# Streaming encoder step on one core: first weights laid out by block with their squares summed on TensorE, the norm's columns between a sublayer's first two units, weight splits ordered behind the norm, early gate weights

## The chip, the cores and the metric

The kernel runs on one core of a Trainium2 chip. The metric is the device time of one execution in microseconds (us). Of the kernel before, three runs were timed: 965.52, 967.45 and 967.6 us, median 967.45. One more execution was recorded by the hardware profiler; the trace and its page come from it.

In the text, TensorE is PE in the profile (PEld its weight loads), VectorE is DVE, ScalarE is ACT, GpSimd is POOL, and SP is the engine that issues the loads from memory.

## The reference

One step of a two-layer encoder over 288 tokens (256 of a prompt, 32 of a sample with caches), 1024 features. Each layer has three sublayers, each on a normed copy of the stream `x` and added back to it:

```python
def rmsnorm(x, g):
    xf = x.astype(jnp.float32)
    y = xf * lax.rsqrt(jnp.mean(xf * xf, axis=-1, keepdims=True) + RMS_EPS)
    return (y * g.astype(jnp.float32)).astype(x.dtype)
...
def memory_attn(h, mk, mv, w_q, w_o):
    ...
    return o.reshape(b, t, D_MODEL) @ w_o

def swiglu(h, w_gate, w_up, w_down):
    return (jax.nn.silu(h @ w_gate) * (h @ w_up)) @ w_down
```

In layer 0 the first sublayer is a chunked attention and a stick-breaking attention side by side (`mix_ab`); in layer 1 it is a forgetting attention whose scores get a bias from the cumulated logarithm of 16 gates (`mix_c`). Then come cross-attention into 256 memory tokens (`cross`) and a gated feed-forward part with 22 x 128 hidden features (`ffn`). A last norm gives the output.

## The kernel before, in words

**Layout.** Features lie on the 128 partitions, tokens along the row: `x` is eight tiles of 128 x 288. A weight matrix comes in units of 128 x 1024 (512 KB), eight blocks of 128 x 128. `unit` (L169) loads one through SP into `st` (four buffers) and splits it into a rounded part `hi` (a cast on ScalarE, L150; five buffers) and the rest `lo` (a subtraction on VectorE, L151; four buffers). `mm3` (L178) multiplies each block with the activations, which are split the same way into `hh` and `hl`: hi x hh, hi x hl, lo x hh. So a unit is 24 matmuls over 288 columns.

**The norm.** The scale 1/rms is not applied to the activations before the product but to its result. Class `Norm` sums the squares of the eight blocks of `x`: the squares on ScalarE (`sq`, L235), the additions on POOL, the last one on VectorE (`ssq`, L243). `columns` brings the sum across partitions with six small matmuls (`nrm`), then takes the inverse root by Newton's steps on VectorE (`ms`, `y`, `nt`; 11 small instructions, L257 to L262). `rows` spreads it along the tokens with six more matmuls (`nr`), and `scale` copies it to `rstd` on ScalarE (L310). What is to be scaled (`xq` in cross, `gs` and `us` in ffn, `q`, `kv` and the gate's `gz` in mix_c) waits in a list until then.

**The opening of a sublayer.** `begin` (L194) computes the first six blocks of the first two units, for the last two blocks of `x` aren't there yet. `project` finishes each unit. After each finished unit `tick` advances the generators in `active`, `scale` among them: in cross and ffn it does nothing at the first tick, issues `columns` at the second and `rows` at the third, in the two mix sublayers one tick earlier.

**The order.** A scheduler orders the instructions of each engine; each engine then works through its own list. `not_before` adds an order without a wait. `held` (L165) uses it for the two halves of a split, only while `hurry` is set (the first four heads of mix_ab): they stand behind an earlier matmul and behind what `scale` has put into `behind`. Elsewhere splits run ahead as far as the buffers go.

**The start.** SP loads the first three units (`first`) in nine pieces of columns, between the four pieces of `x`. Their blocks are multiplied side by side, in `side_by_side` (L802), and the eight squares are added on VectorE (seven additions, L243) before one group of `nrm`. 32 matmuls of a unit matrix (`warm`, L132) precede all of this.

**Mix_c.** The gate's 32 weight columns (`wg`) are loaded at the opening, multiplied by the gain on VectorE (`wgg`, L944), and used for `gp`. `gate` (L878) turns this into `gz`, transposes with the summing matrix `fold4` (`gt`), and after a chain of small steps into `lf`, from which matmuls make the cumulated bias (`gc`, `gs`, `gn`); it goes to memory and comes back by loads. For each pair of sample heads `sample` loads four strips of it (`bcs`) and four columns (`cq`), subtracts, and masks four strips on POOL (L989). At the end, `turn_early` puts four transposes between the two halves of the last norm's `nrm`.

Of the kernel before, what the change touches and what calls it, by code (L numbers as in the profile page):

```python
# [26 lines left out]
def encoder_step(ctx: ExitStack, tc: tile.TileContext, a):  # L27
# [46 lines left out]

    first = [wp.tile([P, 1024], F32, tag="st", bufs=4, name=f"first{i}") for i in range(3)]

    def first_part(i, c0, c1):
        DMA.dma_start(first[i][:, c0:c1], a["w_ab"][4 * i][:, c0:c1])

    PARTS = ((0, 256), (256, 512), (512, 1024))  # L80
    first_part(0, *PARTS[0])
    for i in range(4):
        DMA.dma_start(xh[i], a["xT"][:, 2 * i * NT:2 * (i + 1) * NT])
        if i == 0:
            DMA.dma_start(gain, a["gains"])
        if i < 3:
            for u in range(3):
                if i or u:
                    first_part(u, *PARTS[i])
# [16 lines left out]
    V.tensor_copy(ntrir, ntri)  # L106
# [27 lines left out]
    V.tensor_scalar(ident, warm[:, 0:P], 1.0 / 32.0, None, op0=ALU.mult)  # L134
    fold = cst.tile([P, 2, 32], F32, name="fold")
    by_head = ident.rearrange("p (j i q) -> p j i q", j=2, i=2)
    V.tensor_tensor(fold, by_head[:, :, 0], by_head[:, :, 1], ALU.add)

    fold4 = cst.tile([P, 16], F32, name="fold4")
    V.tensor_tensor(fold4, fold[:, 0, 0:16], fold[:, 1, 0:16], ALU.add)  # L140
# [53 lines left out]
    def begin(srcs, h):  # L194
# [30 lines left out]
    class Norm:  # L225
# [7 lines left out]
        def add(self, xb, eng=None):  # L233
# [3 lines left out]
            eng = eng or (V if self.parts == KT else G)  # L237
            i = int(self.parts == KT and self.hurry)
            if self.acc[i] is None:
                self.acc[i] = q  # L240
            else:
                s = tok("ssq")
                eng.tensor_tensor(s[:, :self.n], self.acc[i][:, :self.n], q[:, :self.n], ALU.add)  # L243
                self.acc[i] = s

        def columns(self, between=None):
            p = att("nrm")
            c = len(self.tiles)
            for part in self.acc:
                if between and part is self.acc[1]:  # L250
                    between()
                for i, t in enumerate(self.tiles):
                    if part is not None:
                        mm(p[:, 2 * i:2 * i + 2], part[:, t:t + 128], mean1, i == 0 and part is self.acc[0], False)
# [28 lines left out]
    class Next:  # L283


        def __init__(self, gi):
            self.gi, self.norm, self.h, self.waiting = gi, Norm(hurry=gi == 8), ([], []), []

# [213 lines left out]
    def stick_prompt(q, k, v, vns, j, oh, ol):  # L502
# [121 lines left out]
    def cross(layer, cur, memory, nxt):  # L624
        o = ([tok("oh", F32R) for _ in range(KT)], [tok("ol", F32R) for _ in range(KT)])
        q, qs = [], []
        begun = begin([a["w_xq"][layer, f] for f in range(2)], cur.h)
# [101 lines left out]
    def ffn(layer, cur, nxt, ahead):  # L729
# [16 lines left out]
        begun = begin([a["w_gate"][layer, 0], a["w_up"][layer, 0]], cur.h)  # L746
# [50 lines left out]
    def mix_ab(cur, nxt, memory, w0):  # L797
# [3 lines left out]

        def side_by_side():  # L802
            p = [att("pj"), acc("pj"), acc("pj")]
            with tc.issue_after(warmed.ins):
# [8 lines left out]
        biases = {}  # L813
# [64 lines left out]
    def gate(cur, p, res, lf, bf):  # L878
# [10 lines left out]
        z, e, u, l, f = (sm.tile([P, 48], F32, tag="g" + s, bufs=1, name="gate_" + s) for s in "zeulf")  # L889
# [41 lines left out]

    def mix_c(cur, nxt, memory, w0):
        o = ([tok("oh", F32R) for _ in range(KT)], [tok("ol", F32R) for _ in range(KT)])
        cum = []
        lf = cst.tile([P, 64], F32, name="lf")
        not_before(DMA.dma_start(lf[:, 48:64], a["clf"]), loads[-4])
        bf = cst.tile([P, 1], F32, name="bf")
        G.memset(bf, 0.0)
        not_before(DMA.dma_start(bf[0:16], a["b_f"]), loads[-4])

        wg, wgg = tok("wg"), tok("wgg")
        DMA.dma_start(wg[:, 0:256], a["w_g"])
        g = gain[:, KT:2 * KT].unsqueeze(2).to_broadcast([P, KT, 32])
        V.tensor_tensor(wgg[:, 0:256].rearrange("p (k c) -> p k c", c=32), wg[:, 0:256].rearrange("p (k c) -> p k c", c=32), g, ALU.mult)  # L944
        w = a["w_c"]
        begun = begin([w[0], w[8]], cur.h)
        active.append(cur.scale())
        p = acc("gp")
        for k in range(KT):
            mm(p[32 * (k % 4):32 * (k % 4) + 32, :NT], wgg[:, 32 * k:32 * k + 32], x[k], k < 4, k >= 4)  # L950
# [24 lines left out]
        def sample(g):  # L975
# [11 lines left out]
            for h in range(4):  # L987
                pr = slice(32 * h, 32 * h + 32)
                G.affine_select(out=t[pr, 128:160], in_=t[pr, 128:160], pattern=[[-1, NS]], compare_op=ALU.is_ge,  # L989
                                fill=NEG, base=0, channel_multiplier=1)  # L990
            oo = ([o[0][j] for j in two], [o[1][j] for j in two])
            return attend_sample([qs[j] for j in two], [ks[j] for j in two], two, vns, ck, cv, t, oo)
# [6 lines left out]
    w0 = [unit_tiles() for _ in first]  # L999
    for m in range(KT):  # L1000
        cur.block(m, start=True)
        if m in (1, 3, 5):
            for st, w in zip(first, w0):
                split_weights(st, w, *PARTS[m // 2])
    for m in range(KT):
        cur.norm.add(x[m], V)
    memories = [Memory(0), Memory(1)]
    for layer in range(2):
        nxt = Next(2 + layer)
        (mix_ab, mix_c)[layer](cur, nxt, memories[layer], w0)  # L1010
        cur, nxt = nxt, Next(6 + layer)
# [12 lines left out]
    def turn_early():  # L1024
        for m in range(4):
# [3 lines left out]
    for t in range(3):  # L1029
        for m in range(4 if t == 0 else 0, KT):  # L1030
# [21 lines left out]
def _pack(inputs):  # L1052
# [17 lines left out]
    def vals(c):  # L1070
# [4 lines left out]
                      g["g_ffn"][0], g["g_ffn"][1], g["g_final"]])  # L1075
    w_g = np.pad(g["w_in_c"][0][:, 3072:], ((0, 0), (0, 16)))
# [5 lines left out]
        "w_ab": units(g["w_in_ab"][0]), "w_oab": units(g["w_out_ab"][0]),  # L1082
# [41 lines left out]
```

## Time and profile before

| | |
|---|---|
| runs | 965.52, 967.45, 967.6 us; median 967.45 |
| profiled execution | 965.87 us; span in the trace 964.2 us |
| granted TensorE clock | 0.998 |
| TensorE busy | 946.9 us, 98% of the span, 7484 instructions |
| VectorE, ScalarE, POOL busy | 591.0, 485.7, 239.9 us (61%, 50%, 25%) |
| moved by DMA | 160.99 MB, 167 GB/s on average |

A row of the timeline gives the start and the length in us, the engine, the line of the kernel, the operation, and the tile written and those read, with their shapes; in brackets, how long the engine had been idle before, and what released it. A row of the chain gives start, length, engine and tile. Rows with "x" and a number stand for that many instructions in a row. Consecutive instructions of an engine overlap a little, so the distance between starts, not the length of one, is the pace.

### The profile page before, as it was taken

To read this page: it belongs to the slowest core of one execution; us is meant where nothing else is said; L and a number is where in the kernel's file an instruction comes from. 1 tells how busy PE (TensorE), PEld (TensorE's weight loads), DVE (VectorE), ACT (ScalarE), POOL (GpSimd) and SP (SyncE) were. 2 spreads that over 40 slices of the span, in tenths; PEclk is the share of its full clock that TensorE was granted. 3 is DMA by queue.
4 is the path that set the end of the run, shared out by engine and by line. 5 is a ranking of instruction groups with operands and counts; after the bars stand their busy time and mean duration, and the time that the engine had idled before them with its cause. 6 is when DMAs were issued, how large, how long until landed. Compare 5 with 4: busy or idle time off the path is not lost.

```text
span 964.2 us, 19131 instructions
## 1 busy us (share of the span) xinstructions
PE 946.9 (98%) x7484; PEld 914.2 (95%) x7484; DVE 591.0 (61%) x1140; ACT 485.7 (50%) x862; POOL 239.9 (25%) x364
## 2 busy tenths in 40 slices
PE   8999999999999999999989999999999999999997
PEld 7889999999999999999988899999989999999996
DVE  6786556676766555855466666667767655555442
ACT  5566767544554444444345445455546544444331
POOL 3341122300212222410115454423012222222010
PEclk9999999999999999999999999999999999999999
DMA  8666445443354544555456455545425444444531
GB/s 264 202 206 202 142 170 192 167 159 126 122 171 155 175 163 166 176 197 175 165 187 200 159 191 186 165 169 189 157 85 175 154 173 157 174 164 165 175 110 50
DMA packets 50459, 160.99 MB, mean 167 GB/s; under 512 B 7864, under 2 KB 9336, under 8 KB 50368
## 3 DMA queue, kind: packets, MB, share of 16 engines
q1 hardware_dynamic: 46464, 149.71, 45.7%
q0 software_dynamic: 3904, 10.04, 3.0%
q8 instruction: 59, 0.97, 0.4%
q14 instruction: 32, 0.26, 0.1%
HBM read 149.58 MB, written 10.15 MB: 166 GB/s over the span
## 4 chain that ended last, share of the span: by engine, by line
PE 91%; DVE 3%; DMA 2%; ACT 2%; issue 1%; SPq 0%; POOL 0%; DVEq 0%; ACTq 0%; POOLq 0%
PE pj L68 51%; PE dn L68 14%; PE op L68 10%; PE mv L68 5%; PE po L68 1%; PE xo L68 1%; DMA x<-xT 1%; PE zb L68 1%; PE sc L68 1%; PE xs L68 1%; DMA st<-w_ab 1%; DMA wg<-w_g 1%; PE nrm L68 1%; PE xss L68 1%; ACT hi L150 1%
## 5 line engine op out<-in xcount | busy, mean ns | idle before, releaser
L150 ACT CAST hi<-st 128x1024 fp32r<-128x1024 f32 x257 | 269.1, 1050 | 321.9 <-issue 142.8
L68 PE MATMUL pj<-hh,hi 128*128 128x288 f32 (+1 forms) x1344 | 400.9, 298 | 1.1 <-DVE gz L882 1.1
L68 PE MATMUL pj<-hl,hi 128*128 128x288 f32 (+1 forms) x1344 | 395.6, 294 | 0.0
L68 PE MATMUL pj<-hh,lo 128*128 128x288 f32 (+1 forms) x1344 | 394.7, 294 | 0.4 <-DVE lo L151 0.4
L151 DVE TENSOR_TENSOR lo<-st,hi 128x1024 fp32r<-128x1024 f32 x257 | 321.3, 1250 | 116.8 <-PE dn L68 42.7
L68 PEld LDWEIGHTS pj<-hh,hi 128*128 128x128 f32 x1344 | 253.2, 188 | 7.1 <-issue 5.4
L68 PEld LDWEIGHTS pj<-hh,lo 128*128 128x128 f32 x1344 | 253.3, 188 | 1.1 <-DVE lo L151 1.0
L68 PEld LDWEIGHTS pj<-hl,hi 128*128 128x128 f32 x1344 | 253.3, 188 | 0.5 <-issue 0.5
L68 PE MATMUL dn<-fh,hi 128*128 128x288 f32 x400 | 108.6, 294 | 0.0
L68 PE MATMUL dn<-fh,lo 128*128 128x288 f32 x352 | 103.7, 295 | 0.0
L68 PE MATMUL dn<-fl,hi 128*128 128x288 f32 x304 | 89.4, 294 | 0.0
L68 PE MATMUL op<-ol,hi 128*128 128x288 f32 x256 | 75.7, 296 | 0.0
L68 PE MATMUL op<-oh,hi 128*128 128x288 f32 x256 | 75.5, 297 | 0.0
L68 PE MATMUL op<-oh,lo 128*128 128x288 f32 x256 | 75.2, 294 | 0.0
L68 PEld LDWEIGHTS dn<-fh,hi 128*128 128x128 f32 x400 | 72.5, 188 | 0.0
L68 PEld LDWEIGHTS dn<-fh,lo 128*128 128x128 f32 x352 | 66.1, 188 | 0.0
L243 POOL TENSOR_TENSOR ssq<-ssq,sq 128x288 f32<-128x288 f32 (+1 forms) x35 | 36.3, 1036 | 114.8 <-ACT sq L235 72.3
L742 POOL TENSOR_TENSOR fl<-us,fh 128x288 fp32r<-128x288 f32 x38 | 33.0, 868 | 119.2 <-ACT fh L741 116.6
L738 POOL TENSOR_TENSOR gs<-gs,sg 128x288 f32<-128x288 f32 x44 | 38.7, 880 | 74.7 <-ACT sg L736 73.5
L68 PEld LDWEIGHTS dn<-fl,hi 128*128 128x128 f32 x304 | 57.1, 188 | 0.0
L737 DVE TENSOR_TENSOR us<-pj,rstd 128x288 f32<-128x288 f32 x44 | 20.1, 457 | 59.2 <-PE pj L68 59.2
L68 PEld LDWEIGHTS op<-ol,hi 128*128 128x128 f32 x256 | 48.1, 188 | 0.6 <-issue 0.4
(266 smaller groups left out, 1261.4 us busy)
## 6 DMA issues: line engine op xcount, KB each, us to landing
st<-w_gate SPq DMA_DIRECT2D x44, 512.0 KB, 3.2
st<-w_up SPq DMA_DIRECT2D x44, 512.0 KB, 3.2
st<-w_down SPq DMA_DIRECT2D x44, 512.0 KB, 3.2
st<-w_c SPq DMA_DIRECT2D x24, 512.0 KB, 3.3
st<-w_ab SPq DMA_DIRECT2D x21, 512.0 KB, 4.8
st<-w_xk SPq DMA_DIRECT2D x16, 512.0 KB, 3.4
st<-w_xv SPq DMA_DIRECT2D x16, 512.0 KB, 3.7
st<-w_xq SPq DMA_DIRECT2D x16, 512.0 KB, 3.7
```

Source lines behind the costliest of these rows:

```text
L68: return T.matmul(out, lhsT, rhs, start=start, stop=stop, skip_group_check=True)
L150: a = S.copy(hi, st[:, c0:c1])
L151: b = V.tensor_tensor(lo, st[:, c0:c1], hi.bitcast(F32), ALU.subtract)
L243: eng.tensor_tensor(s[:, :self.n], self.acc[i][:, :self.n], q[:, :self.n], ALU.add)
L737: V.tensor_tensor(us, pu[:, :NT], cur.r, ALU.mult)
L738: G.tensor_tensor(gs, gs, sg, ALU.mult)
L742: G.tensor_tensor(lo, us, hi.bitcast(F32), ALU.subtract)
```

## The change

- **First weights.** The host lays out blocks of the first three units in the order in which they are used (`w_first`): eight steps of three blocks. They come in four loads (of 384, 640, 1024 and 1024 columns) between the pieces of `x`, and are split in seven parts.
- **First norm.** The eight squares are not added: `Norm.sum` puts six `nrm` matmuls for each, from the third step of `side_by_side` on, so that TensorE accumulates them.
- **Columns earlier.** `begin` calls `columns` after the first unit's six blocks, for every sublayer but the first; `scale` issues `rows` at its first tick.
- **Splits held.** `scale` now fills `behind` in every sublayer: first Newton's last step, and one tick later the copy to `rstd` and the last evacuation. `held` orders every split behind the last three entries, for those on its own engine.
- **Gate.** `wg`, `lf`'s cached columns and `bf` are loaded after mix_ab, the multiplication by the gain is on POOL, `gp` takes a bank of the other pool. The five gate tiles are one tile.
- **Mix_c's samples.** Two loads for each pair instead of eight, one addition of a mask made once (`mnew`) instead of four selections, and one tick more before the scores.
- **Small ones.** The two mask matmuls of each `zb` become one; some constants (`ident`, `fold`, `fold4`, `ntrir`) are written later on VectorE; `turn_early` makes two transposes instead of four.

```diff
+    first_part(0, 0, 384)
+    x_part(0)
+    DMA.dma_start(gain, a["gains"])
+    first_part(0, 384, 1024)
+    x_part(1)
+    first_part(1, 0, 1024)
+    x_part(2)
+    first_part(2, 0, 1024)
+    x_part(3)
...
     def held(ins):
-        if hurry[0]:
-            for i in began[-2:-1] + [i for i in behind if i.engine == ins.ins.engine]:
-                not_before(ins, i)
+        for i in (began[-2:-1] if hurry[0] else []) + [i for i in behind[-3:] if i.engine == ins.ins.engine]:
+            not_before(ins, i)
...
             for k in range(BEGIN):
-                mm3(p[:, :NT], w, k, h, k, k == 0, False)
+                mm3(p[:, :NT], w, k, cur.h, k, k == 0, False)
             out.append((w, p))
+            if len(out) == 1:
+                cur.y = cur.norm.columns()
         return out
...
+        def sum(self, p, part, begin):
+            for i, t in enumerate(self.tiles):
+                mm(p[:, 2 * i:2 * i + 2], part[:, t:t + 128], mean1, begin and i == 0, False)
...
         def scale(self):
 
-            if self.gi > 1:
+            if self.gi == 0:
                 yield 1
-            y = self.norm.columns()
-            yield 1
-            p = self.norm.rows(y)
+            p = self.norm.rows(self.y)
...
-            if self.gi == 0:
-                behind.append(self.norm.last.ins)
-                yield 1
-                behind.extend([r.ins, done[-1].ins])
+            behind.append(self.norm.last.ins)
+            yield 1
+            behind.extend([r.ins] + [d.ins for d in done[-1:] if d is not None])
...
-            mm(z[:, 0:128], identb, mdiag, False, False)
-            mm(z[:, 256:384], identb, mdiag, False, False)
+            mm(z[:, 0:512].rearrange("p (t q) -> p t q", q=256)[:, :, 0:128], identb, mdiag.unsqueeze(1).to_broadcast([P, 2, P]), False, False)
...
-                        i = mm3(p[u][:, :NT], w0[u], k, cur.h, k, k == 0, k == KT - 1)
+                        b = 3 * k + u
+                        i = mm3(p[u][:, :NT], w0[b // 8], b % 8, cur.h, k, k == 0, k == KT - 1)
                         if k in (0, 5, 7) and u == 2:
                             began.append(i.ins)
+                    if k > 1:
+                        cur.norm.sum(sums, squares[k - 2], k == 2)
+            for q in squares[KT - 2:]:
+                cur.norm.sum(sums, q, False)
+            cur.y = cur.norm.newton(sums)
...
+    def gate_inputs():
+
+        for t, src in ((lf[:, 48:64], a["clf"]), (bf[0:16], a["b_f"]), (wg, a["w_g"])):
+            not_before(DMA.dma_start(t, src), loads[-1])
+        G.tensor_tensor(wg, wg, gain[:, KT:2 * KT].unsqueeze(2).to_broadcast([P, KT, 32]), ALU.mult)
...
-        begun = begin([w[0], w[8]], cur.h)
+        begun = begin([w[0], w[8]], cur)
         active.append(cur.scale())
-        p = acc("gp")
+        p = att("gp")
...
-            for h in range(4):
-                off = sp.offset + 160 * (4 * g + h)
-                pr = slice(32 * h, 32 * h + 32)
-                DMA.dma_start(t[pr, 0:160], bass.AP(tensor=sp.tensor, offset=off, ap=[[0, NS], [1, 160]]))
-                DMA.dma_start(cq[pr, 0:1], bass.AP(tensor=sp.tensor, offset=off + 128, ap=[[1, NS], [1, 1]]))
+            off = sp.offset + 160 * 4 * g
+            DMA.dma_start(t[:, 0:160], bass.AP(tensor=sp.tensor, offset=off, ap=[[160, 4], [0, NS], [1, 160]]))
+            DMA.dma_start(cq[:, 0:1], bass.AP(tensor=sp.tensor, offset=off + 128, ap=[[160, 4], [1, NS], [1, 1]]))
             G.tensor_tensor(t[:, 0:160], cq[:, 0:1].to_broadcast([P, 160]), t[:, 0:160], ALU.subtract)
...
+            G.tensor_tensor(t[:, 128:160], t[:, 128:160], mnew, ALU.add)
+            yield 1
```

**The order on ScalarE, opening of layer 0's cross.** In the rows before, `hh` and `sq` belong to the last blocks of the projection ahead of it, `rstd` is the norm's copy, `qh` the casts of the first queries, and `hi` the casts of this sublayer's units:

```order
L150 CAST hi_2771<-st_2769 128x1024
L277 ACTIVATE hh_2570<-x_82,gain 128x288
L235 ACTIVATE sq_2574<-x_82 128x288
L150 CAST hi_2838<-st_2836 128x1024
L277 ACTIVATE hh_2610<-x_82,gain 128x288
L235 ACTIVATE sq_2614<-x_82 128x288
L150 CAST hi_2895<-st_2893 128x1024
L150 CAST hi_2975<-st_2973 128x1024
L150 CAST hi_3031<-st_3029 128x1024
L310 COPY rstd_2749<-nr_2745 128x288
L349 CAST qh_2753<-xq_2751 128x256
```

The same place in the changed kernel, from the last blocks' `hh` and `sq` on:

```order
L291 ACTIVATE hh_2565<-x_82,gain 128x288
L243 ACTIVATE sq_2569<-x_82 128x288
L291 ACTIVATE hh_2605<-x_82,gain 128x288
L243 ACTIVATE sq_2609<-x_82 128x288
L323 COPY rstd_2724<-nr_2720 128x288
L156 CAST hi_2746<-st_2744 128x1024
L361 CAST qh_2728<-xq_2726 128x256
L361 CAST qh_2740<-xq_2738 128x256
L156 CAST hi_2783<-st_2781 128x1024
```

Five casts that stood ahead of the copy have moved behind it; `hi_2746` is that of the third unit. VectorE has the same in the changed kernel, with Newton's last step (`y`), the scaled queries (`xq`) and the third unit's `lo_2747`:

```order
L276 SCALAR_TENSOR_TENSOR y_2676<-nt_2677,y_2676 128x6
L656 SCALAR_TENSOR_TENSOR xq_2726<-pj_2652,rstd_2724 128x288
L656 SCALAR_TENSOR_TENSOR xq_2738<-pj_2695,rstd_2724 128x288
L157 TENSOR_TENSOR lo_2747<-st_2744,hi_2746 128x1024
L362 TENSOR_TENSOR ql_2729<-xq_2726,qh_2728 128x256
```

The third unit's `lo` has come to stand behind two queries. **The order on TensorE** at that place in the changed kernel: `nr` is the rows group, `pj_2695` the last two blocks of the second unit, `pj_2750` the third unit, `xs` the scores of the first head:

```order
L68 MATMUL nr_2720<-ident,y_2676 128x128 x2
L68 MATMUL nr_2720<-ident,y_2676 128x32
L68 MATMUL pj_2695<-hh_2565,hi_2691 128x288
L68 MATMUL pj_2695<-hl_2566,hi_2691 128x288
L68 MATMUL pj_2695<-hh_2565,lo_2692 128x288
L68 MATMUL pj_2695<-hh_2605,hi_2691 128x288
L68 MATMUL pj_2695<-hl_2606,hi_2691 128x288
L68 MATMUL pj_2695<-hh_2605,lo_2692 128x288
L68 MATMUL pj_2750<-hh_2377,hi_2746 128x288
L68 MATMUL pj_2750<-hl_2378,hi_2746 128x288
L68 MATMUL xs_2812<-kh_1257,qh_2728 128x256
L68 MATMUL xs_2812<-kl_1258,qh_2728 128x256
```

Between `nr` and the third unit stand the six last matmuls of the second. **At the start**, the end of the side-by-side blocks on TensorE, before:

```order
L68 MATMUL pj_285<-hh_233,hi_185 128x288
L68 MATMUL pj_285<-hl_234,hi_185 128x288
L68 MATMUL pj_285<-hh_233,lo_186 128x288
L68 MATMUL nrm_358<-mean_100,ssq_265 128x2 x3
L68 MATMUL pj_393<-hh_187,hi_389 128x288
```

and in the changed kernel, where `sq` are squares of single blocks of `x`:

```order
L68 MATMUL pj_267<-hl_236,hi_181 128x288
L68 MATMUL pj_267<-hh_235,lo_182 128x288
L68 MATMUL nrm_268<-mean_95,sq_239 128x2 x3
L68 MATMUL nrm_268<-mean_95,sq_241 128x2 x3
L68 MATMUL nrm_268<-mean_95,sq_243 128x2 x3
L68 MATMUL pj_396<-hh_183,hi_392 128x288
```

Five more groups of this kind stand between the earlier steps. Each row with x3 is six matmuls in the trace.

More of the change, by code (lines that the diff above doesn't have):

```diff
@@ L77, in first_part, with x_part @@
     def first_part(i, c0, c1):
[L78 to L82, printed above, removed]
+        DMA.dma_start(first[i][:, c0:c1], a["w_first"][i][:, c0:c1])
+    def x_part(i):
         DMA.dma_start(xh[i], a["xT"][:, 2 * i * NT:2 * (i + 1) * NT])
[L84 to L89, printed above, removed]
+    first_part(0, 0, 384)
[7 more added lines that the diff above has]
+    x_part(3)
     mean1 = cst.tile([P, 2], F32, name="mean1")
@@ L888, in gate @@
         mm(t[0:NS, 32:48], zt[:, 256:288], fold4)
-        z, e, u, l, f = (sm.tile([P, 48], F32, tag="g" + s, bufs=1, name="gate_" + s) for s in "zeulf")
+        five = tok("gate")
+        z, e, u, l, f = (five[:, 48 * i:48 * i + 48] for i in range(5))
         G.memset(z, 0.0)
@@ L934, in mix_c @@
         cum = []
[L935 to L944, printed above, removed]
         w = a["w_c"]
[L946 removed]
+        begun = begin([w[0], w[8]], cur)
         active.append(cur.scale())
[L948 removed]
+        p = att("gp")
         for k in range(KT):
[L950 removed]
+            mm(p[32 * (k % 4):32 * (k % 4) + 32, :NT], wg[:, k], x[k], k < 4, k >= 4)
         cur.then(lambda: start(gate(cur, p, cum, lf, bf)))
@@ L999, in encoder_step, with square @@
     w0 = [unit_tiles() for _ in first]
+    parts = iter([(0, 0, 384), (0, 384, 768), (0, 768, 1024), (1, 0, 512), (1, 512, 1024), (2, 0, 512), (2, 512, 1024)])
+    squares = []
+    def square(m):
+        squares.append(tok("sq"))
+        S.activation(squares[m], x[m], AF.Square)
     for m in range(KT):
         cur.block(m, start=True)
[L1002 to L1006, printed above, removed]
+        for i, c0, c1 in [p for _, p in zip(range((1, 1, 2, 0, 1, 1, 1, 0)[m]), parts)]:
+            split_weights(first[i], w0[i], c0, c1)
+        if m > 1:
+            square(m - 2)
+    square(KT - 2)
+    square(KT - 1)
+    more_constants()
     memories = [Memory(0), Memory(1)]
@@ L1024, in turn_early @@
     def turn_early():
-        for m in range(4):
+        for m in range(2):
             turn(0, m)
@@ L1029, in encoder_step @@
     for t in range(3):
-        for m in range(4 if t == 0 else 0, KT):
+        for m in range(2 if t == 0 else 0, KT):
             turn(t, m)
```

58 lines of the change are left out of this document (35 added, 23 removed).

## The prediction

> **What bounds the kernel now.** I read the table of busy times first, then the chain that ended last, the costliest groups, a stretch in the middle, and TensorE's list of waits.
>
> ```profile
> PE 946.9 (98%) x7484; PEld 914.2 (95%) x7484; DVE 591.0 (61%) x1140; ACT 485.7 (50%) x862; POOL 239.9 (25%) x364
> PE 91%; DVE 3%; DMA 2%; ACT 2%; issue 1%; SPq 0%; POOL 0%; DVEq 0%; ACTq 0%; POOLq 0%
> L150 ACT CAST hi<-st 128x1024 fp32r<-128x1024 f32 x257 | 269.1, 1050 | 321.9 <-issue 142.8
> L151 DVE TENSOR_TENSOR lo<-st,hi 128x1024 fp32r<-128x1024 f32 x257 | 321.3, 1250 | 116.8 <-PE dn L68 42.7
> 280.00:320.00 40.00, 40.00 (x306) 39.98 (x305) 24.60 (x41) 19.85 (x28) 11.09 (x14) 1.00 0.50 169
> 282.44 129.75 PE pj L68 x982
> ```
>
> TensorE is busy for 98% of the span; from 280 to 320 us (the window's row: length, then busy time of PE, PEld, DVE, ACT, POOL, then granted clock) for 40.00 of 40.00 us at clock 1.00. Its pace is 129.75 / 982 = 0.132 us a matmul, so a unit of 24 takes 3.17 us. To split a unit costs ScalarE 1.05 and VectorE 1.25 us: both have room on average. Only two things can move the end: work added to TensorE, and time in which it stands. Standing is rare (each row: who waits for what, us in total, times, longest):
>
> ```profile
> PE warm L132 <- POOL identb masks.py:199: 2.6, 1, 2.6
> PE gp L68 <- DVE wgg L944: 1.3, 1, 1.3
> PE pj L68 <- DVE gz L882: 1.1, 1, 1.1
> PE nrm L68 <- DVE ssq L243: 1.1, 1, 1.1
> PE ts L441 <- DVE es L389: 0.8, 1, 0.8
> PE gc L68 <- DVE lf L904: 0.6, 1, 0.6
> PE nr L68 <- DVE y L262: 0.2, 1, 0.2
> ```
>
> The change goes at nearly every row here. But no row names a wait at the opening of the two cross sublayers and the two ffns, and the change touches those too. Against the profiled execution (965.87 us, span 964.2) I sum six terms.
>
> **1. The start.** Removed: 7 adds on VectorE and the wait behind them, and the waits for the third parts of the weights. Added: 7 more groups of six norm matmuls.
>
> ```profile
> 5.92 0.59 PE L68 MATMUL pj<-hh,hi 128*128 128x288 f32 x1
> 12.25 0.36 PE L68 MATMUL pj<-hh,lo 128*128 128x288 f32 x1
> ...
> 14.52 0.29 PE L68 MATMUL pj<-hh,hi 128*128 128x288 f32 x1
> 15.98 3.27 DVE L243 TENSOR_TENSOR ssq<-ssq,sq 128x288 f32<-128x288 f32 x6
> 19.31 0.83 PE L68 MATMUL nrm<-mean,ssq 128*128 128x2 f32 x6 [1.06 <-DVE ssq L243]
> 20.14 3.51 PE pj L68 x24
> 199.43 0.56 PE nrm L68 x6
> ```
>
> An undisturbed group costs TensorE 0.56 us (0.093 a matmul, for two columns of result), so seven cost 3.9. Gone are the wait of 1.06 and its group's slow start (0.83 - 0.56 = 0.27). Between 12.25 and 14.52 seven steps from matmul to matmul take 2.27 us where 7 x 0.132 = 0.92 would do: the third parts' splits come late there, by 1.35 in all, and those blocks now come in other pieces. I take it that nothing waits in their place except perhaps the first block of the second load (0 to 0.4). TensorE still starts at about 5.92, since the 32 warming matmuls stand before it. Sum: 3.9 - 1.3 - 1.4 = **+1.2**. Bounds: +0.3, if half of the added time falls into waits that come anyway, to +2.0, if the old part waits come back in another place.
>
> The Trainium skill, "TensorE: Matmul & The Clock Gate", section "Back-to-back issue gap", says that the spacing of a stream of weight loads and matmuls is set by both, and gives about 81 ns with 128 columns streamed; by that a group of six, which stream two columns each, would be an estimated 0.49 us at most and the start 0.5 us shorter. The row has 0.56, which I use.
>
> **2. The two cross openings.** Before, `held` ordered splits only in the first four heads. Now each split stands behind the last step of the norm: the cast `hi` behind the copy of rstd on ScalarE, `lo` behind Newton's last step and then the evacuations on VectorE. Before, five casts stood ahead of that copy; now the third unit's comes after it. The norm itself moves up by one unit, so that between the rows matmuls and the third unit TensorE has only six matmuls.
>
> ```profile
> 193.06 6.37 PE pj L68 x48
> 195.03 0.45 DVE L243 TENSOR_TENSOR ssq<-ssq,sq 128x288 f32<-128x288 f32 x1
> 203.18 1.05 ACT L150 CAST hi<-st 128x1024 fp32r<-128x1024 f32 x1 [2.64 <-PE pj L68]
> 203.54 0.66 PE nr L68 x6
> 204.23 0.40 ACT L310 COPY rstd<-nr 128x288 f32<-128x288 f32 x1
> 204.66 1.19 DVE L645 SCALAR_TENSOR_TENSOR xq<-pj,rstd 128x288 f32<-128x288 f32 x3
> ```
>
> Count from the start of the rows matmuls (nr). TensorE: 0.66 + 6 x 0.132 = 1.45, then it wants `hi` of unit 3. ScalarE: rstd starts at 204.23 - 203.54 = 0.69 and takes 0.40, then the cast takes 1.05: ready at about 2.1. Stall 0.6. Then two matmuls of the unit and two of the scores, and TensorE wants `lo`, without stalls at 1.45 + 4 x 0.132 = 1.96. VectorE: the first xq from 204.66 - 203.54 = 1.12; the second needs the end of unit 2's last matmul at about 1.65 and ends at 2.1 (1.19 / 3 = 0.40 each, more when alone); `lo` then takes 1.25: 3.35. All in all 3.35 - 1.96 = 1.4 each: **+2.8**. Bounds 1.0 (`hi` and `lo` overlap with what is ahead of them) to 1.8 each. The sum of squares is no new wait: its last add ended 195.48 - 193.06 = 2.42 us after the projection before, and the 18 matmuls that now stand ahead of nrm take 2.38; a split that delayed that add has moved behind it besides.
>
> **3. The two ffn openings.**
>
> ```profile
> 281.80 0.64 PE nr L68 x6
> 282.48 0.40 ACT L310 COPY rstd<-nr 128x288 f32<-128x288 f32 x1
> 282.89 1.28 ACT L736 ACT_TABLE_LOAD   x1
> 282.91 0.46 DVE L735 TENSOR_TENSOR gs<-pj,rstd 128x288 f32<-128x288 f32 x1
> 283.28 0.45 DVE L737 TENSOR_TENSOR us<-pj,rstd 128x288 f32<-128x288 f32 x1
> ```
>
> The same, with gs and us in place of the two xq and no scores matmuls: `lo` is there at about 3.35, TensorE wants it at 1.45 + 2 x 0.132 = 1.72. Stall **1.65** each, **+3.3**. Bounds 1.3 to 2.0: the table load of 1.28 stands behind the third unit's cast and delays the gate product and so the fourth unit's `lo`, which by the same count is ready within 0.2 of its turn.
>
> **4. Mix_c's opening.** Gone: the waits for wgg (1.3), gz (1.1) and y (0.2), since w_g is loaded and scaled a sublayer earlier, in POOL's idle time, and the copies no longer meet a split. With lf's 0.6 that is 3.2 by the list, 3.7 with the slower matmul after each.
>
> ```profile
> 495.11 0.84 PE nr L68 x6
> 496.40 0.47 DVE gz L882
> 497.94 0.52 PE gt L68 x6
> ```
>
> New: VectorE has gz, q, gz's bias and kv (four of about 0.4 from 1.15, to 2.6), then waits for the gate transposes to copy (to 3.4), then `lo`: ready at 4.65. TensorE wants it at 2.85 (nr, six matmuls, two of unit 3, gt, four of the memory units). Stall 1.8. The gate's chain moves with it and lf stays late by about 0.7. Together 2.5 (2.7 with restarts) against 3.7: **-1.0**. Bounds -2.4 (no stall but lf) to 0.
>
> **5. Mix_c's first sample heads.**
>
> ```profile
> 531.86 1.07 POOL L989 TENSOR_SCALAR_AFFINE_SELECT bcs<-bcs 32x32 f32<-32x32 f32 x4
> 532.96 0.32 DVE L384 CUSTOM_DVE_ANT_0 es<-ss,bcs 128x160 f32<-128x160 f32 x1 [0.36 <-POOL bcs L989]
> 534.44 0.33 PE L441 MATMUL ts<-ident,es 128*128 128x128 f32 x1 [0.77 <-DVE es L389]
> ```
>
> Two loads instead of eight, one add instead of four selects, and a unit more between scores and bias: the wait of 0.77 goes, **-0.8** (bounds -1.0 to 0).
>
> **6. Nothing.** The merged mask matmuls stream the same columns; the constants built later on VectorE are first needed after the start; the gate's tiles and mnew are POOL's work, 25% busy; if POOL's scaling of w_g waited for its load, only the adds of squares would queue behind it, two units ahead of their use. At the tail the last norm matmuls stand behind the same nine transposes.
>
> Sum: 1.2 + 2.8 + 3.3 - 1.0 - 0.8 = **+5.5**. The profiled execution becomes 971.4; it lay 1.6 below the median of the runs shown (967.45, from 965.52 to 967.6). Adding 5.5 to the median gives 973.0; I forecast **972.3** between.
>
> **The rivals.** *A, faster: the openings are covered.* If casts and subtractions of unit 3 got done within the 1.45 us, terms 2 and 3 vanish and the first part of 4: 1.2 - 2.8 - 0.8 = -2.4, 965.1. It decides at a delay from nr to `hi` of 1.45 and to `lo` of 1.72 to 1.96 us; for it, that no opening waits now, and ScalarE idles 2.64 us before the cast at 203.18. Against it, rstd's own row already ends at 1.09 and a cast is 1.05. It needs a queue other than the written one. 0.1.
>
> *B: the start is a gain.* The norm groups fall into time in which TensorE would wait for loads anyway, or cost less between other matmuls: with a third of their 3.9 left, the start is 1.3 - 2.7 = -1.4 in place of +1.2, the total +2.9, 969.7.
>
> ```profile
> 0.00:20.00 20.00, 15.99 (x111) 15.00 (x111) 12.67 (x29) 13.15 (x29) 8.50 (x34) 1.00 0.84 257
> 2.57 3.59 PE L132 MATMUL warm<-identb 128*128 128x128 bf16 x32 [2.57 <-POOL identb masks.py:199]
> ```
>
> For it, the loads run at 257 GB/s here and TensorE idles 4 of 20 us; against it, most of that is ahead of 5.92 and in the waits already counted. 0.15. The Trainium skill, "TensorE: Matmul & The Clock Gate", section "Back-to-back issue gap", has a floor of about 25 ns for an isolated matmul of up to 64 columns as well; by that a group would be an estimated 0.15 us and the start about 1.6 us shorter than before. The row's 0.56 us agree with what it says of streams, not with that floor.
>
> *C: the openings cost more.* The queues come out of the first stall with no lead, and the fourth and fifth units stall too, by 0.5 to 0.8 at each of five openings: +3, 975.3. For it, the ffn's table load and gate product ahead of the fourth `lo`; against it, both engines need 1.25 per 3.17 us after it. 0.2.
>
> *D: it does not do what it says*: the openings' order binds nothing, and the start's gains and costs cancel: within 0.2% of 967.45. 0.05.
>
> **How the numbers follow.** My forecast has 0.5, A 0.1, B 0.15, C 0.2, D 0.05. With all bounds of terms 1 to 5 at one end the sum would move by -4 or +4; as they hardly come together I take -2.8 to +2.7, so the forecast's own range is 969.5 to 975. Taking in B and C, and leaving out most of A, the range is 967.3 to 976.0. About 0.2%, 1.9 us, is what a measurement of this kernel can tell from no change. Faster by more: A, 0.1. Within: D and the low end of B, 0.08. Slower: 0.82.
>
> **What would show it.** Right: the list of waits names `hi` (about 0.6) and `lo` (about 0.8 to 1.8) of the third unit at five places, just after rstd; nrm's groups at the start take about 0.56 each and the first unit after them begins at about 21.3, not 20.14; wgg, gz and es vanish from the list. Wrong: no wait for `hi` or `lo` after the start, or stalls of over 2.5 us at an opening, or a sum of squares that ends before 20.

## The result and the profile after

| | before | changed |
|---|---|---|
| runs | 965.52 to 967.6 us, median 967.11 of 4 | 977.54 to 978.98 us, median 978.36 of 4 |
| profiled execution | 965.87 us, span 964.2 | 977.54 us, span 975.8 |
| granted TensorE clock | 0.998 | 0.998 |

The ratio is 1.0119 (95% interval 1.0101 to 1.0136): the change costs 11.3 us. The prediction had the sign, but said 972.3 and at most 976.0.

First TensorE's list of waits in the changed kernel, in the same form as before:

```profile
PE pj L68 <- ACT hi L156: 3.2, 6, 0.6
PE pj L68 <- DVE lo L157: 2.8, 6, 0.7
PE warm L134 <- POOL identb masks.py:199: 2.6, 1, 2.6
PE xt L672 <- DVE xe L401: 2.1, 4, 0.8
PE tp L421 <- DVE e L401: 1.3, 4, 0.6
PE gc L68 <- DVE lf L923: 1.2, 1, 1.2
PE tp L422 <- DVE e L401: 0.3, 1, 0.3
PE pj L68 <- ACT hh L291: 0.2, 1, 0.2
PE pj L68 <- DVE hl L294: 0.2, 1, 0.2
```

The waits for wgg, gz and es are gone, as forecast, and six waits each for `hi` and `lo` have come: all those for `hi` and five of those for `lo` at the openings (mix_c's has two for `hi`), one for `lo` at the start. What was not forecast is the row for xe, the first softmax's result, and lf's is larger than forecast (1.2, before 0.6). The row for xe in the kernel before:

```profile
PE xt L661 <- DVE xe L389: 0.7, 2, 0.3
```

The list does not add up to 11.3, since it counts neither the slower matmul after a wait nor work that TensorE has gained. A table by stage does better. It is read off the timelines of the two profiled executions: the start of the first rows matmul, then the distances between the starts of the last `op` matmul of an out projection and of the first and last `dn` matmul of an ffn.

| stage, us | before | changed | difference | forecast |
|---|---|---|---|---|
| start, to the first nr | 23.48 | 26.10 | +2.6 | +1.2 |
| rest of mix_ab | 169.28 | 168.93 | -0.4 | 0 |
| cross, layer 0 | 78.27 | 81.50 | +3.2 | +1.4 |
| ffn, gate and up, layer 0 | 140.98 | 143.22 | +2.2 | +1.65 |
| ffn, down, layer 0 | 69.73 | 69.62 | -0.1 | 0 |
| mix_c | 182.24 | 182.34 | +0.1 | -1.8 |
| cross, layer 1 | 78.11 | 81.23 | +3.1 | +1.4 |
| ffn, gate and up, layer 1 | 141.16 | 142.10 | +0.9 | +1.65 |
| ffn, down, layer 1 | 69.52 | 69.74 | +0.2 | 0 |

Layer 0's cross at its opening, TensorE, ScalarE and VectorE of the timeline (in each row start and length, in brackets the idle time before it and what ended it):

```profile
201.39 0.75 PE L68 MATMUL nr<-ident,y 128*128 128x128 f32 x6
203.58 0.40 PE L68 MATMUL pj<-hh,hi 128*128 128x288 f32 x1 [0.55 <-ACT hi L156]
204.84 0.40 PE L68 MATMUL pj<-hh,lo 128*128 128x288 f32 x1 [0.45 <-DVE lo L157]
```

```profile
202.18 0.40 ACT L323 COPY rstd<-nr 128x288 f32<-128x288 f32 x1 [5.46 <-PE nr L68]
202.47 1.05 ACT L156 CAST hi<-st 128x1024 fp32r<-128x1024 f32 x1
```

```profile
202.61 0.91 DVE L656 SCALAR_TENSOR_TENSOR xq<-pj,rstd 128x288 f32<-128x288 f32 x2 [2.14 <-ACT rstd L323]
203.56 1.23 DVE L157 TENSOR_TENSOR lo<-st,hi 128x1024 fp32r<-128x1024 f32 x1
```

The bracket at rstd is the point: ScalarE had been idle for 5.46 us, and VectorE before xq for 2.14, with the third unit's cast and subtraction next in their queues. From the rows matmuls to `lo` it is 204.84 - 201.39 = 3.45 us; the prediction had counted 3.35. The opening itself went as forecast. What follows it did not. Here is the first softmax, on TensorE, ScalarE and VectorE:

```profile
216.34 0.30 PE L672 MATMUL xt<-ident,xe 128*128 128x128 f32 x1 [0.78 <-DVE xe L401]
```

```profile
210.82 1.05 ACT L156 CAST hi<-st 128x1024 fp32r<-128x1024 f32 x1 [1.16 <-DMA st<-w_xq]
212.72 1.05 ACT L156 CAST hi<-st 128x1024 fp32r<-128x1024 f32 x1 [0.85 <-DMA st<-w_xv]
213.68 0.40 ACT L361 CAST qh<-xq 128x256 fp32r<-128x256 f32 x1
213.99 0.47 ACT L393 ACTIVATE xe<-xs,st 128x256 f32<-128x256 f32 x1
```

```profile
211.91 1.23 DVE L157 TENSOR_TENSOR lo<-st,hi 128x1024 fp32r<-128x1024 f32 x1 [0.21 <-ACT hi L156]
213.05 0.42 DVE L392 TENSOR_REDUCE st<-xs 128x1 f32<-128x256 f32 x1
```

The scores end at 212.2 on TensorE. In the kernel before, the first reduction began 0.3 us after them; here it begins 0.85 after them, behind a `lo`, and the exponential stands behind two casts that waited for their loads. The late third split, and those queued behind it, gave their buffers back late, so the loads came late, so splits of later units arrive just when the softmax wants the same two engines. In e1 below, without the hold, no cast of this stretch waits for a load.

### The profile page after: what moved, and what is told of

The parts are those of the page before. It is cut to its first block, busy times and chain, and to the rows that moved or that the text cites. A ratio compares the mean times of both kernels' runs of the same rounds, so it can differ in the third digit from the quotient of the medians.

```text
span 975.8 us, 19112 instructions
## 1 busy us (share of the span) xinstructions
PE 954.7 (98%) x7518; PEld 917.7 (94%) x7518; DVE 592.5 (61%) x1130; ACT 483.9 (50%) x860; POOL 237.5 (24%) x358
## 4 chain that ended last, share of the span: by engine, by line
PE 91%; DVE 4%; ACT 2%; DMA 1%; issue 1%; SPq 0%; DVEq 0%; ACTq 0%
PE pj L68 51%; PE dn L68 14%; PE op L68 10%; PE mv L68 5%; DVE lo L157 2%; PE po L68 1%; PE xo L68 1%; PE sc L68 1%; PE zb L68 1%; PE nrm L68 1%; ACT hi L156 1%; PE xs L68 1%; PE xss L68 1%; DMA x<-xT 1%; PE xt L672 1%
## 5 line engine op out<-in xcount | busy, mean ns | idle before, releaser
L753 POOL TENSOR_TENSOR fl<-us,fh 128x288 fp32r<-128x288 f32 x38 | 35.2, 926 | 121.2 <-ACT fh L752 121.2
L251 POOL TENSOR_TENSOR ssq<-ssq,sq 128x288 f32<-128x288 f32 (+1 forms) x35 | 33.4, 955 | 112.5 <-ACT sq L243 65.6
```

Of the source, the lines that this page charges most:

```text
L753: G.tensor_tensor(lo, us, hi.bitcast(F32), ALU.subtract)
```

## The experiments

Each was timed in five rounds against the kernel before on its own chip. Since chips differ a little (the kernel before had medians from 965.88 to 967.11), ratios are compared, and stages as in the table above. The stages come from one execution each, and in four of these executions the granted TensorE clock was halved for about 3.4 us. Here is that stretch in e5_old_start, g2_four_groups, f1_third_free and g1_gate_only, as rows of the window view (the window and its length, busy time of PE, PEld, DVE, ACT and POOL, then the granted clock, the DMA share and GB/s):

```profile
20.80:24.30 3.50, 3.50 (x16) 3.50 (x17) 2.83 (x13) 0.00 (x0) 0.00 (x0) 0.51 0.66 234
20.80:24.30 3.50, 3.50 (x17) 3.50 (x16) 2.29 (x8) 0.00 (x0) 0.00 (x0) 0.51 0.18 70
508.90:512.30 3.40, 3.40 (x18) 3.40 (x17) 1.79 (x4) 1.45 (x2) 1.31 (x2) 0.50 0.30 113
507.15:510.56 3.41, 3.41 (x18) 3.41 (x18) 0.52 (x2) 0.41 (x1) 1.31 (x2) 0.50 0.63 201
```

In e5 the 24 matmuls behind `nrm` take 4.64 us with the drop and in before 3.48 without one, in g2 4.81 and in e2 3.46. So a drop costs some 1.2 to 1.5 us, and a stage that holds one is longer by that. It also shows in the mean clock of an execution: 0.996 or 0.997 for these four profiled ones, 0.998 or 0.999 for the other nine. Where it matters below, the timed executions with a mean clock of at least 0.998 are compared as well.

**e1_no_hold**, the changed kernel with the old condition in `held`:

```diff
-        for i in (began[-2:-1] if hurry[0] else []) + [i for i in behind[-3:] if i.engine == ins.ins.engine]:
-            not_before(ins, i)
+        if hurry[0]:
+            for i in began[-2:-1] + [i for i in behind[-3:] if i.engine == ins.ins.engine]:
+                not_before(ins, i)
```

> The changed kernel with splits held as before (only in mix_ab's first four heads); all else as changed. Theory: the order behind an early norm makes the openings slow (1.3 to 1.6 us of hi and lo waits at each of five, and about 1.2 at the first softmax of each cross). Then some 8 to 9 us go and 969 to 970 is left; hi and lo vanish from TensorE's list of waits, and xe has 0.7 again, not 2.1. Rival: the norm's earlier place itself costs the time, held or not: 975 or more, with waits at the same places.

Measured: 967.26 us, ratio 1.001 (0.9998 to 1.0023). Nearly all of the change's 11 us are gone, more than the 8 to 9 expected. The stages: cross 78.52 and 78.30, ffn 141.54 and 141.23, mix_c 179.84. From its list of waits:

```profile
PE tp L423 <- DVE e L402: 0.7, 2, 0.4
PE xt L673 <- DVE xe L402: 0.6, 2, 0.4
PE gc L68 <- DVE lf L924: 0.6, 1, 0.6
PE tp L422 <- DVE e L402: 0.6, 2, 0.3
PE vt L378 <- DVE kv L789: 0.5, 1, 0.5
PE pj L68 <- DVE lo L157: 0.2, 1, 0.2
```

No `hi`, and one `lo` at the start; xe and lf are back at 0.6. The rival, that the early norm itself costs it, has fallen. By stages the hold costs 2.9 to 3.0 in each cross, 1.7 and 0.9 in the ffns and 2.5 in mix_c.

**e3_before_hold**, the kernel before with the hold alone, columns and rows in their late places (the edits to `held` and to the end of `scale`, nothing else):

> The kernel before, with only the order of the splits behind the norm in every sublayer; columns and rows stay in their late places. Theory: holding costs only together with the early norm, since with the late one it is the fourth unit that is held, and TensorE has some 20 matmuls of the third left after the rows: 967 to 968.5. Rival: holding alone costs it, early norm or not: 972 or more.

Measured: 966.71 us, ratio 0.9997 (0.9986 to 1.0008). The hold alone costs nothing that can be measured in the total. (One of its twelve executions took 2348.16 us; it is left out of the ratio, and its cause is not known.) By stages the crosses are 0.7 longer than before (78.97 and 78.81), ffn 140.94 and 141.08 and mix_c 182.22 the same; the stages ahead of the first cross came out 0.9 shorter, where all engines have the kernel before's order, so that is scatter; by the ratio's interval a price of 0.8 us is not excluded. So neither edit costs the 11 us by itself, only the two together: with the early norm the held unit is the third, and TensorE has six matmuls left.

**f1_third_free**, the changed kernel with the first unit after `begin` exempt from the hold:

```diff
-        split_weights(st, w, hold=True)
+        third, fresh[0] = fresh[0], False
+        split_weights(st, w, hold=not third)
...
+        fresh[0] = True
         return out
```

> The changed kernel, except that the third unit of a sublayer (the first after the two that begin it) is not held; all later units are. Theory: only the third unit is too late for TensorE, and the later waits (xe in the cross, lf in mix_c) follow from its stall: within 1 us of e1's 967.3, no hi or lo in the list of waits, xe at 0.6 to 0.8. Rival: the held later units fill the queues too; then 969 to 973, with xe at 1.5 or more and waits for lo of the fourth unit in the ffns.

Measured: 968.76 us, ratio 1.0032 (1.0012 to 1.0052). That lies between the two theories' ranges. As the first had it, the openings are free of waits, with cross at 78.98 and 78.94 and ffn at 141.38 and 140.81. But xe and lf stay late, as the rival had it:

```profile
PE xt L674 <- DVE xe L403: 1.6, 4, 0.6
PE gc L68 <- DVE lf L925: 1.4, 1, 1.4
PE pj L68 <- DVE lo L157: 0.2, 1, 0.2
```

By the ratios, freeing the third unit takes away 1.0119 - 1.0032, or 8.4 us; the later held units, which stand among softmax and gate, keep 1.0032 - 1.001, or 2.1. Part of these 2.1 is the clock. The drop of this execution lies in mix_c: 16 matmuls follow each other at 0.21 us where the next ones take 0.12, about 1.5 us of its 182.14 (179.84 in e1). The six executions with a mean clock of at least 0.998 have a median of 967.86, e1's seven, on another chip, 966.85: by these the later units keep about 1 us. The converse needs no run: with the hold on the third unit alone, the order on all five engines is that of the changed kernel, since the later splits queue up behind it.

**h_lo_only**, the changed kernel with only the subtraction held:

```diff
         if hold:
-            held(a)
-            held(b)
+            for ins in ((a, b) if hurry[0] else (b,)):
+                held(ins)
```

> The changed kernel with only the subtractions (lo) held, the casts (hi) free. In its order lo of the third unit stands right behind Newton's last step, ahead of the scaled queries. Theory: the cast behind rstd is what makes both late, since lo cannot start before hi; with casts free lo is there about 0.9 us after the rows matmuls start, before TensorE wants it: 966.5 to 968.5, no hi or lo in the waits. Rival: lo alone, behind Newton, still costs over 0.5 at each opening: 970 to 974.

Measured: 967.58 us, ratio 1.0012 (1.0001 to 1.0024), as e1. So the cast behind rstd on ScalarE is what costs; `lo` is late because `hi` is. ScalarE and VectorE of the opening:

```profile
202.41 1.05 ACT L156 CAST hi<-st 128x1024 fp32r<-128x1024 f32 x1 [4.73 <-PE pj L68]
203.36 0.39 ACT L323 COPY rstd<-nr 128x288 f32<-128x288 f32 x1
```

```profile
201.34 3.49 DVE L157 TENSOR_TENSOR lo<-st,hi 128x1024 fp32r<-128x1024 f32 x3
204.75 0.82 DVE L656 SCALAR_TENSOR_TENSOR xq<-pj,rstd 128x288 f32<-128x288 f32 x2
```

Three subtractions have run before the first xq, and nothing waits for xq in time to matter.

**e2_dve_squares**, e1 with the squares added on VectorE between the blocks, one group of norm matmuls, and the new loads kept:

```diff
-                    if k > 1:
-                        cur.norm.sum(sums, squares[k - 2], k == 2)
-            for q in squares[KT - 2:]:
-                cur.norm.sum(sums, q, False)
+            cur.norm.sum(sums, total[0], True)
```

> As e1, but the eight squares are added on VectorE again, with one group of norm matmuls; the new loads of the first weights stay. If the seven added groups are what the start costs (3.9 less the wait of 1.3 that comes back), it is 2 to 3 us faster than e1. Rival: the new loads cost it; then it is within 0.5 us of e1 or slower, with waits for hh, hl and hi near 9 to 11 us.

Measured: 961.5 us, ratio 0.9942 (0.9929 to 0.9955), 5.5 us faster than before and 5.8 faster than e1, twice what was expected. The first rows matmul starts at 22.03, in e1 at 25.78, before at 23.48; the rest of mix_ab takes 168.44, in e1 169.50. From the list of waits of e2, which has no ssq in it:

```profile
PE xt L673 <- DVE xe L402: 0.7, 2, 0.3
PE gc L68 <- DVE lf L921: 0.6, 1, 0.6
PE tp L423 <- DVE e L402: 0.6, 2, 0.3
PE tp L422 <- DVE e L402: 0.6, 2, 0.3
PE pj L68 <- DVE lo L157: 0.2, 1, 0.2
```

So the sum needs no TensorE: put between the blocks as the squares come, with the new loads, the seven additions on VectorE are hidden. The old loads with the additions between the blocks were not tried.

**g2_four_groups**, e2 with the squares added in pairs and four groups of norm matmuls at the end:

> As e2, with the squares added in pairs on VectorE and four groups of norm matmuls instead of one (eight in e1, at the end of the side-by-side blocks instead of between them). Theory: each group costs TensorE about 0.65 us, three more make 2.0: 963.5. Rival: e1 loses its 5.8 to e2 by where the groups stand, not by their number: within 0.7 of e2's 961.5.

Measured: 965.1 us, ratio 0.9986 (0.9975 to 0.9998). Three groups more cost 0.0044 of the time, 4.2 us, twice what was expected. By the stages 2.6 of it stand at the start (first nr at 24.61) and 0.9 in the second ffn, which has nothing to do with the edit (below). But the four groups take 2.59 us, from 17.21 to 19.80, and e2's one 0.69, which is 0.63 for each group more, as the theory had it; 1.35 more at the start are the clock drop in the unit behind them. The three executions with a mean clock of at least 0.998 have a median of 963.74, 1.8 below such executions of the kernel before on their chip, and e2's five 961.5, 4.1 below: 2.3 us for three groups. The number of groups counts, at 0.63 to 0.77 us each.

**e5_old_start**, e1 with the start as before (nine loads, additions on VectorE at the end):

> As e1, with the start as before (loads in nine pieces, squares added on VectorE): what is left of the change is the early norm, the gate's early inputs, the samples and the small edits. Theory: the start cost 2.6 us, so 2.6 less than e1, about 966.5, a little under before for mix_c's opening. Rival: the start's cost is covered elsewhere, and e5 equals e1 within 0.7 us.

Measured: 964.04 us, ratio 0.997 (0.9958 to 0.9982). That is 3.2 faster than e1, where 2.6 was expected, but in the profiled execution not by the route expected: its first nr is at 25.94, no earlier than e1's 25.78, and it gains 1.3 in the rest of mix_ab (168.23). The clock drop lies in this start and takes 1.2 us of it, ssq is waited for 1.4 us and a `hi` 0.9. Against before it loses 2.5 at the start and gains 1.1 in the rest of mix_ab and 2.5 in mix_c (179.70). The loss is not the code's: all engines run before's instructions there in before's order, as they do in e3 and g1, whose first nr came at 23.10 and 23.97. All five executions of e5 had a mean clock of 0.996 or 0.997, so its time holds a drop throughout.

**g3_new_start**, the kernel before with e2's start:

> The kernel before, with only e2's start: the four loads laid out by block, the splits in seven parts, the squares taken and added on VectorE between the blocks, the constants later. Theory: the start is 1.5 shorter by the first rows matmuls of e2 and before (22.0 and 23.5): 964.5 to 965.5. Rival: mix_ab gives it back in its first heads, whose weights come no earlier: within 0.7 of before.

Measured: 964.65 us, ratio 0.9985 (0.997 to 0.9999). First nr at 21.75, 1.7 earlier than before; mix_c happens to take 0.7 longer (182.95). The new loads with the additions between the blocks are worth 1.4 to 1.7 us.

**f3_late_norm**, e2 with columns and rows in the old places:

> As e2 (new loads, squares added on VectorE, no hold), with columns and rows in the late places of the kernel before. Theory: without the hold TensorE waits for the norm in neither place, so the early norm is worth nothing: 961 to 962.5, against e2's 961.5. Rival: the early norm is what makes e2 and e5 faster than before: 963 or more.

Measured: 962.61 us, ratio 0.9959 (0.9945 to 0.9973), against e2's 0.9942: 1.1 us slower in the medians, with intervals that overlap. The stages put 0.9 of it in mix_c (181.06 against 180.16), where lf is waited for 1.5 instead of 0.6; cross (78.24, 78.02) and the first ffn (140.92) are no slower. So the early norm is worth nothing in cross and ffn, and about 1 us in mix_c.

**g1_gate_only**, the kernel before with the gate's inputs loaded early:

> The kernel before, with only the gate's inputs loaded after mix_ab, the gain multiplied in on POOL, gp in a bank of the other pool and one gate tile. Theory: the wait for wgg goes (1.3, 1.8 with the slow matmul after it), the others of mix_c's opening stay with the late norm: 1.5 to 1.8 less than before. Rival: w_g was late only because TensorE came early; the wait moves to gz or nr and the gain is under 0.7.

Measured: 965.64 us, ratio 1.0001 (0.9989 to 1.0012): nothing. Its list says where part of the gain went:

```profile
PE gc L68 <- DVE lf L905: 1.5, 1, 1.5
PE nrm L68 <- DVE ssq L243: 1.1, 1, 1.1
PE pj L68 <- ACT hi L150: 1.0, 2, 0.9
PE ts L441 <- DVE es L389: 0.8, 1, 0.8
```

The waits for wgg, gz and y have gone, but lf, the end of the gate's chain, now has 1.5 instead of 0.6 (the `hi` is at the start), and mix_c takes 181.97 against 182.24. Most of the rest went into the clock: up to the first `gn` mix_c is 1.6 us shorter than before (24.9 instead of 26.5), and then comes the drop, with 15 matmuls at 0.21 us where the next ones take 0.12. Ten of g1's eleven executions have a mean clock of 0.997 or less, of the kernel before on the same chip 9 of 27; the eleventh took 963.69, against 965.58, the median of the other 18. So as timed the edit gains nothing; without the drop it gains about 1.5 to 1.9 by this stage and that one execution, as the theory had it. Whether the longer wait for lf brings the drop was not tried. Early gate weights, early norm and free splits together give 2.1 to 2.5 in mix_c (e1, e2, e5), and early gate weights with the late norm 1.2 (f3, where no clock dropped).

**f4_old_samples**, e2 with mix_c's sample heads as before:

> As e2, with mix_c's sample heads as before (eight loads, four selections, no added tick). By the prediction's term the wait of 0.8 for es comes back: 962.3. Rival: the added tick cuts TensorE's stretches of small matmuls in two, which costs as much as the wait: within 0.4 us of e2's 961.5.

Measured: 961.14 us, ratio 0.9941 (0.9925 to 0.9957), as e2. The wait for es is back:

```profile
PE ts L454 <- DVE es L402: 0.8, 1, 0.8
```

and still mix_c takes 179.89 against 180.16. The new form saves the wait and pays as much elsewhere. In the changed kernel's timeline the scores of the sample heads stand by themselves, no longer behind the prompt's; each change between the two kinds of matmul costs TensorE 0.2 to 0.3 us. That this is the price was only read from the trace, not tried.

## Why the prediction was right in its sign and too small

Term 2, the cross: the mechanism was right and the opening's size too (3.45 us from rows to `lo`, counted 3.35). The step that failed is that the term ended at the opening. Rival C spoke of a backlog after the first stall, "the fourth and fifth units stall too"; what stalled was the first softmax (xe, 2.1 us in the list instead of 0.7) and the small matmuls cut apart around it: some 1.6 more in each cross. In layer 0, from the unit behind the scores to the first `xt` it takes 4.1 us, in e1 3.2, and `xt` and `xss` together take 2.25, in e1 1.56. With the hold removed (e1) all of it went, and with the third unit free (f1) all but 0.5 to 0.6.

Term 3, the ffns: right in sum, 3.3 forecast and 2.2 + 0.9 measured. The waits are alike in both (0.57 and 0.73 us in each). Against e1, which has the same pace in layer 0's long stretch after them (6.360, explained below), the opening costs 1.7, as counted; in layer 1 the changed kernel's pace is faster than e1's (6.307 against 6.347), which hides 0.9 of it.

Term 4, mix_c's opening: the waits went and new ones came, but lf was put at 0.7 late and is 1.2, and the gain of 1.0 did not show: +0.1 for the sublayer as a whole. The cost was sized right, 2.5 counted and 2.5 taken by the hold (e1). The step that failed is the gain: 3.7 counted here and 0.8 in term 5, and without the hold 2.1 to 2.5 measured (e1, e2, e5). Of the difference 0.6 is lf, still waited for in e1 and e2, and 0.8 is term 5; the rest stays open.

Term 5, the samples: -0.8 forecast. The wait went, the time did not (f4). The step that failed is "the wait goes" taken for "the time goes".

Term 1, the start: +1.2 forecast, +2.6 measured in these two executions. With the changed kernel's start, the first nr came at 25.32 (f1), 25.63 (h_lo_only), 25.78 (e1) and 26.10; with before's at 23.10 (e3), 23.48 and 23.97 (g1), e5 with its clock drop aside. On average that is +2.2. Two steps failed. The price of a norm group was taken from one that stands alone between matmuls, 0.56; in the changed kernel

```profile
11.54 0.72 PE L68 MATMUL nrm<-mean,sq 128*128 128x2 f32 x6
12.12 0.38 PE L68 MATMUL pj<-hh,hi 128*128 128x288 f32 x1
12.34 0.29 PE L68 MATMUL pj<-hl,hi 128*128 128x288 f32 x1
```

a group takes 0.58 and the matmul behind it 0.22 instead of 0.13: 0.67 in all, so 4.7 for seven where 3.9 was counted. And "nothing waits in their place except perhaps the first block of the second load" missed the waits for hh and hl of the third block and hi and lo of the second load (8.97 to 11.3 us), 1.4 in all beyond the usual pace, of which only the last two were thought of, at 0 to 0.4. Of the two waits that the change took away, that for ssq needed no TensorE at all (e2).

Of the rivals, A and D fell with the first list of waits. B, that the start gains, is true of the new loads with the additions between the blocks (g3) and false of the squares on TensorE (e2 against e1): the two edits of the start had opposite signs, and the prediction added them into one. No account had that the hold costs next to nothing where it stands alone (e3).

The Trainium skill, "TensorE: Matmul & The Clock Gate", section "Back-to-back issue gap", was cited for a spacing set by weight load and matmul together, at about 81 ns with 128 columns; the groups here have 0.097 us a matmul (0.58 / 6), the matmul behind them 0.09 us on top, which its figures do not include.

What stays open: e1 and e2 differ by 5.8 us, of which 3.75 stand at the start and 1.1 in the rest of mix_ab; why that rest depends on the start was not tried. Best of all kernels run are e2 and f4, both 0.6% faster than before; by executions with a mean clock of at least 0.998, all of theirs and 11 and 16 of before's, 4.1 and 4.7 us.

## What to carry to other kernels

An order that keeps work behind a norm costs little as long as the bound engine has more left to do than the held work takes, and dear as soon as it has not; moving the norm earlier moves that line, so count from the norm to the first use of what is held, and then look at who shares the engines with the late work, not only at the first stall. A wait that is removed is only worth what is not late next: early gate weights, early norm and free splits gave over 2 us together, and early gate weights alone, as timed, nothing. When one edit has two parts, price and try them apart: here a good start of loads and additions hid a bad sum on TensorE. And look at the granted clock in narrow windows before a stage is read from one execution.

## What the runs showed of the hardware that was not expected

The granted clock can halve for about 3.4 us in the middle of a kernel that keeps TensorE busy for 98% of the span, as in the four windows shown ahead of the experiments. In the 3.4 us before each drop TensorE had waited 1.4 to 1.5 us, for ssq in e5 and for lf in f1 and g1, or run 24 matmuls of two columns (g2). The length of a wait does not decide it alone: f3 waits 1.5 us for lf and e3 1.8 for wgg, with no drop. What does was not tried. The clock row of the page shows none of the four.

The pace of a long undisturbed stretch is not the same in all kernels, at the same granted clock. In the gate and up units of the ffns, from 25 us after their opening to their end, 48 matmuls take on average 6.338 us in the kernel before in layer 0 and 6.347 in layer 1 (starts of the first and last matmul, divided), 6.360 and 6.307 in the changed one, and up to 6.387 in g2's second ffn; e3, e5 and g1 have before's 6.338 and 6.347 within 0.001, in spite of edits elsewhere. Over the 116 us of such a stretch 0.05 in 6.34 is 0.9 us. So a stage can differ by 1 us between kernels without any wait, which is as large as several of the terms weighed here.

At the very start, TensorE's matmuls follow each other at 0.24 us until about 8.5 us and at 0.13 from there on, although 32 warming matmuls have run since 2.6 us:

```profile
6.54 0.44 PE L68 MATMUL pj<-hh,lo 128*128 128x288 f32 x1
6.78 0.44 PE L68 MATMUL pj<-hh,hi 128*128 128x288 f32 x1
...
8.64 0.30 PE L68 MATMUL pj<-hh,lo 128*128 128x288 f32 x1
8.77 0.30 PE L68 MATMUL pj<-hh,hi 128*128 128x288 f32 x1
```

These rows are of the kernel before; the page's clock row shows nothing of it. The moment is not fixed: in e3, e5 and g1, with the same instructions in the same order here, the pace of 0.13 first comes at 8.2, 7.3 and 6.1 us, and in the changed kernel at 6.2.
